# Scattering a PEER gate as two float32r parts in one product of 256 columns, with the one-hots scaled on GpSimd

## The chip, the cores and the metric

The kernel runs on one core of a Trainium2 chip. The metric is the device time of one execution in microseconds, the median of several. Engines are named as in the profile: PE is TensorE (PEld its weight loads), DVE is VectorE, ACT is ScalarE, POOL is GpSimd, and SP issues the transfers.

## What is computed

Four decoder layers work on 256 tokens of 1024 features. Each layer has an attention mixer (sliding window, dilated, latent, then sliding window again), a layer norm, a PEER channel mixer, and a second layer norm. The change touches the PEER mixer only:

```python
q = (t @ w_q).reshape(n_tok, 8, 2, 128)
sc = einsum('thpd,hpkd->thpk', q, keys)            # 128 keys per half
s_top, i_top = top_k(sc, 16)
cand = s_top[:, :, 0, :, None] + s_top[:, :, 1, None, :]
best, sel = top_k(cand, 16)                         # of 16 x 16 sums
idx = take(i_top[..., 0] * 128 + i_top[..., 1], sel)
gate = softmax(best)                                # 8 heads x 16 per token
h = gelu(einsum('cd,ced->ce', t, u[idx]))
y = einsum('ce,ced->cd', gate * h, v[idx])
```

There are 16384 experts in a 128 x 128 grid. The kernel does not gather them: it computes the hidden units of all experts for all tokens, multiplies them by a dense table of gates that is zero where an expert was not chosen, and multiplies by all of v.

## The kernel before

Matrix products that need accuracy are made of float32r parts: a weight chunk of 128 x 1024 is loaded into a raw tile (`_load`, on SP, three buffers), ACT rounds it to its high part (line 88), and DVE, or POOL for a share of the chunks (`pool_share`), subtracts to get the low part (line 94). `split_to` runs this two chunks ahead of use. A projection (`proj_t`, line 121) is then 3 x 8 matmuls of 256 columns: high by high, low by high, high by low.

One PEER layer (`peer`) has these stages, in an order that is written out by hand:

1. Scores (`peer_scores`): 16 projections of w_q chunks, products with the keys, and a copy into `sc`.
2. The hidden-unit loop, 128 iterations, one grid row of u each. Each iteration splits a chunk, projects it, and ACT applies GELU into the table G, which has the row first and the token last (G0 for rows 0 to 63, G1 for the rest).
3. The output loop, 128 iterations over v: ACT and DVE split a row of G (lines 961, 962), and PE accumulates y in four PSUM banks (lines 131 to 135).
4. The last rows with the layer norm (`sum_norm`), which adds y to x.

Beside stages 1 and 2 a generator yields small pieces of other work, and `pace` takes from it as much as a budget allows. First it is `topk_gen`: DVE finds the top 16 and the gates and writes `tab`, 128 x 3 x 256: for each of the 128 picks (partition) and each token its grid row, its grid column and its gate. `tab` is a tile of its own. When `topk_gen` ends, `weights_gen` takes its place until the end of stage 2, at `67 / (125 - j)` pieces per iteration. Of the 128 iterations of a layer, 57 come before any gate is there.

`weights_gen` turns `tab` into dense gates, four tokens (a unit) at a time, 64 units a layer. `build` makes two one-hot tiles, 128 picks by 4 tokens by 128 positions, with one compare on DVE (line 869), and multiplies the second by the gates on DVE (line 871). For each token PE multiplies the two, in plain f32 with 128 columns (line 885), which gives that token's 128 x 128 gate grid in PSUM; the trace holds two records for each such product. Units rotate through four PSUM banks. One iteration later `keep` uses the grid: rows of G that are not computed yet get the gates by a copy on ACT (line 910), and one more iteration later the rows that are computed are multiplied by them on DVE, with one input in PSUM (line 917). Where gates are there already when a row is computed, GELU goes to a temporary tile (line 941) and DVE multiplies into G afterwards (line 924, the late multiply).

SBUF is full but for little: x (128 x 2 x 1024) is held from one norm to the next though a PEER layer reads it only at its end, in the norm; its transposed parts zh and zl feed the projections.

Of the kernel before, what the change touches and what calls it, by code (L numbers as in the profile page):

```python
# [10 lines left out]
F32 = mybir.dt.float32  # L11
F32R = mybir.dt.float32r
# [3 lines left out]
AF = mybir.ActivationFunctionType  # L16
OP = mybir.AluOpType
# [4 lines left out]
T = 256  # L22
# [19 lines left out]
class Kernel:  # L42
# [674 lines left out]
            self.paced -= c  # L717
        return False

    def peer_scores(self, i):  # L720
        nc = self.nc
        keys = self.carve(16, 128)
        qT = self.ring(4, T)
        nc.sync.dma_start(keys, self.a["peer_keys"][i])

        def scores(hp2):
            p = self.small((128, 2, 2, 128))
            for q in range(2):
                hp = 2 * hp2 + q
                for t in range(2):  # L730
                    nc.tensor.matmul(p[:, t, q, :], qT[hp % 4][:, t * 128:t * 128 + 128], keys[:, hp, :],
                                     start=True, stop=True)
            nc.scalar.activation(self.sc[:, :, 2 * hp2:2 * hp2 + 2, :], p, AF.Copy)

        for hp in range(16):
            self.xproj(qT[hp % 4])
            if hp % 2 == 0 and hp:
                scores(hp // 2 - 1)
                self.sc_ready = hp - 2
            self.pace(1.3)  # L740
        scores(7)
        self.sc_ready = 16

    def topk_gen(self, tab):

        nc = self.nc
        V = nc.vector
# [28 lines left out]
        for t in range(2):  # L776
# [3 lines left out]
            f = sif.rearrange("p (h q) k -> p h q k", q=2)  # L780
# [68 lines left out]
            yield 0.2  # L849
        yield 0  # L850
        yield 0
        for t in range(2):
            p = self.small((128, 4, 128))
            for q in range(3):
                nc.tensor.transpose(p[:, q, :], stk[:, t, q, :], self.ident)
            V.tensor_copy(tab[:, 0:3, t * 128:t * 128 + 128], p[:, 0:3, :])
            yield 0.2

    def weights_gen(self, tab, keep):

        nc = self.nc
        V = nc.vector
        shape = [128, 2, 4, 128]
        units = {}

        def build(u):
            ts = slice(4 * u, 4 * u + 4)
            ab = self.misc.tile(shape, F32, name="wk", bufs=2)
            V.tensor_tensor(ab, self.iota[:, None, None, :].to_broadcast(shape),  # L869
                            tab[:, 0:2, ts][:, :, :, None].to_broadcast(shape), op=OP.is_equal)  # L870
            V.tensor_mul(ab[:, 1], ab[:, 1], tab[:, 2, ts][:, :, None].to_broadcast([128, 4, 128]))  # L871
            units[u] = ab

        build(0)
        yield 1
        kept, due = None, None
        for u in range(66):
            if u + 1 < 64:
                build(u + 1)
            p = None  # L880
            if u < 64:
                p = self.ps.tile([128, 4, 128], F32, name=f"y{u % 4}", bufs=1)
                ab = units.pop(u)
                for k in range(4):
                    nc.tensor.matmul(p[:, k, :], ab[:, 0, k, :], ab[:, 1, k, :], start=True, stop=True)  # L885
            if due is not None:
                due()
            due = keep(4 * u - 4, kept.rearrange("p t j -> p j t")) if kept is not None else None
            kept = p
            yield 1  # L890

    def peer(self, i, turn):
        nc = self.nc
        self.new_work()
        tab = self.misc.tile([128, 3, T], F32, name="tab", bufs=1)
        self.sc = self.carve(2, 16, 128)
        self.sc_ready, self.paced = 0, 0.0
        self.side = self.topk_gen(tab)
        self.pool_share = 0.2
        self.peer_scores(i)  # L900
        G = [self.big.tile([128, 64, T], F32, name="G0", bufs=1), None]
        done = [0, 0]

        def keep(t0, p):

            ts = slice(t0, t0 + 4)
            n = [min(max(done[0] - 64 * f, 0), 64) for f in range(2)]
            for f in range(2):
                if n[f] < 64:
                    nc.scalar.activation(G[f][:, n[f]:64, ts], p[:, 64 * f + n[f]:64 * f + 64, :], AF.Copy)  # L910
            done[1] = t0 + 4

            def due():
                for f in range(2):
                    if n[f]:
                        g = G[f][:, 0:n[f], ts]
                        nc.vector.tensor_mul(g, g, p[:, 64 * f:64 * f + n[f], :])
            return due

        started = False  # L920
        late = iter(())

        def times(g, tmp, td):
            nc.vector.tensor_mul(g[:, 0:td], g[:, 0:td], tmp[:, 0:td])
            yield 1

        rate = 1.3
        for j in range(128):
            hi, lo = self.r8(self.nxt())
            ps = self.hps()  # L930
            self.proj_t(ps, hi, lo, self.zh, self.zl, 8)
            if j == 64 and not started:
                self.pace(9999)
                G[1] = self.big.tile([128, 64, T], F32, name="G1", bufs=1)
            next(late, 0)
            late = iter(())
            g = G[j // 64][:, j % 64, :]
            td = done[1]
            if td:
                tmp = self.misc.tile([128, T], F32, name="gtmp", bufs=2)  # L940
                nc.scalar.activation(tmp[:, 0:td], ps[:, 0:td], AF.Gelu)  # L941
                if td < T:
                    nc.scalar.activation(g[:, td:T], ps[:, td:T], AF.Gelu)
                late = times(g, tmp, td)
            else:
                nc.scalar.activation(g, ps, AF.Gelu)  # L946
            done[0] = j + 1
            if self.pace(rate) and not started:
                started = True
                self.pool_share = 0.2  # L950
                if G[1] is None:
                    G[1] = self.big.tile([128, 64, T], F32, name="G1", bufs=1)
                self.side, self.paced = self.weights_gen(tab, keep), 0.0
                rate = 67.0 / (125 - j)
        next(late, 0)
        self.pace(9999)

        def split_g(j):
            gz = self.misc.tile([128, 4, T], F32R, name="wk", bufs=2)
            g = G[j // 64][:, j % 64, :]  # L960
            nc.scalar.activation(gz[:, 0, :], g, AF.Copy)  # L961
            nc.vector.tensor_sub(gz[:, 1, :], g, gz.bitcast(F32)[:, 0, :])  # L962
            return gz[:, 0, :], gz[:, 1, :]

        self.pool_share = 0.0
        self.y = self.psy()
        n = 128 - YTAIL
        z = split_g(0)
        for j in range(n):
            hi, lo = self.nxt(min(SPLITAHEAD, n - 1 - j))  # L970
            if j == n - 1:
                self.new_z()
                for k in range(YTAIL - 3):
                    self.split_to(self.n_use + k, [q[:, 4 * k:4 * k + 4].rearrange("p a b -> p (a b)")
                                                   for q in (self.zh, self.zl)])
            zn = split_g(j + 1) if j < n - 1 else None
            self.proj_n(self.y, hi, lo, z[0], z[1], j == 0, False)
            z = zn
            if j == 67:
                self.new_aux()  # L980
            if j in (68, 71, 74, 77):
                k = (j - 68) // 3
                self.load_norms(i, nc.sync, slice(k, k + 1))
            if j in (80, 83, 86, 89):
                k = (j - 80) // 3
                self.load_biases(i + 1, nc.sync, slice(k, k + 1))
            if j >= 100:
                self.mask_biases(1)
        w = []
        for k in range(0, YTAIL, 2):  # L990
            m = min(2, YTAIL - k)
            if m == 2:
                gz = self.misc.tile([128, 2, 2, T], F32R, name="wk", bufs=2)
                gh, gl = gz[:, 0], gz[:, 1]
            else:
                gh, gl = [self.misc.tile([128, 1, T], F32R, name="gtmp", bufs=2) for _ in range(2)]
            g = G[1][:, 64 - YTAIL + k:64 - YTAIL + k + m, :]
            nc.scalar.activation(gh, g, AF.Copy)
            nc.vector.tensor_sub(gl, g, gh.bitcast(F32))  # L999
            for q in range(m):  # L1000
                w.append(self.nxt(min(SPLITAHEAD, YTAIL - 1 - k - q)) + (gh[:, q], gl[:, q]))
        self.sum_norm(w, False, True, self.ln_slice(0), turn)
# [209 lines left out]
```

## Time and profile before

| | us |
|---|---|
| median of 3 executions | 3997.79 |
| lowest to highest | 3996.78 to 3998.18 |
| the profiled execution | 4000.66 |
| its span | 3998.8 |
| PE busy | 3934.8 |
| DVE busy | 3017.9 |
| ACT busy | 1894.6 |
| POOL busy | 336.1 |

The profile is one execution. A busy engine runs an instruction of the kernel; its durations overlap within PE, so that the spacing of starts tells more about PE than the length of one matmul. DVE instructions overlap a little too: the next starts when the one before is nearly over. An instruction that is held by something other than a semaphore shows it as a longer duration. Stretches are counted from the span's start; the granted clock of 1.00 is TensorE at 2.4 GHz. Below, a line of order of time is the start, the length and the instruction, several alike merged with their count.

### The profile page before, as it was taken

How to read it: one execution, taken by the hardware profiler on the slowest of the kernel's cores; microseconds unless marked ns; L12 is line 12 of the kernel's file. 1: busy time of each engine (PE TensorE's matmuls, PEld its weight loads, DVE VectorE, ACT ScalarE, POOL GpSimd, SP SyncE). 2: the span in 40 equal slices, each digit the busy share in tenths (PEclk: the TensorE clock that was granted, in tenths of full speed). 3: DMA queues.
4: the chain of work that ended last, by engine and by line, in shares of the span. 5: the costliest groups of instructions: out<-in, count | busy, mean ns of one | idle time of the engine just before them, and what ended most of it. 6: DMA issues, size and time to landing. Idle time of an engine off the chain costs nothing. (4 is left out here: it accounts for less than half of the span.)

```text
span 3998.8 us, 68740 instructions
## 1 busy us (share of the span) xinstructions
PE 3934.8 (98%) x26592; PEld 3579.7 (90%) x26592; DVE 3017.9 (75%) x5798; ACT 1894.6 (47%) x3568; POOL 336.1 (8%) x135
## 2 busy tenths in 40 slices
PE   8999999999999999999999999999999999999999
PEld 6999998888998999988887999998888899998887
DVE  7888985566667989965557888985566788996555
ACT  5444444445554444444445444434445444444444
POOL 0111110000001111100000111110000111110000
PEclk9999999999999999999999999999999999999999
DMA  5454445564444554455653554445564455445554
GB/s 182 161 185 151 143 148 187 203 215 156 140 143 143 175 174 143 138 169 189 215 182 105 169 183 152 143 142 187 197 221 148 143 181 168 143 138 175 189 199 159
DMA packets 188007, 668.00 MB, mean 167 GB/s; under 512 B 20688, under 2 KB 27408, under 8 KB 187168
## 3 DMA queue, kind: packets, MB, share of 16 engines
q1 hardware_dynamic: 187424, 663.46, 49.8%
q8 instruction: 209, 3.42, 0.3%
q14 instruction: 118, 0.97, 0.1%
q0 software_dynamic: 64, 0.08, 0.0%
q10 hardware_dynamic: 192, 0.07, 0.0%
HBM read 662.46 MB, written 1.07 MB: 166 GB/s over the span
## 5 line engine op out<-in xcount | busy, mean ns | idle before, releaser
L94 DVE TENSOR_TENSOR lo<-raw,hi 128x1024 fp32r<-128x1024 f32 x1083 | 1324.3, 1223 | 825.4 <-ACT hi L88 821.7
L88 ACT ACTIVATE hi<-raw 128x1024 fp32r<-128x1024 f32 x1212 | 1281.3, 1058 | 724.6 <-PE y L135 696.3
L121 PE MATMUL hp<-zh,hi 128*128 128x256 f32 x5360 | 784.5, 289 | 2.5 <-ACT zh L222 1.7
L121 PE MATMUL hp<-zh,lo 128*128 128x256 f32 x5360 | 752.6, 283 | 0.0
L121 PE MATMUL hp<-zl,hi 128*128 128x256 f32 x5360 | 751.3, 283 | 0.0
L121 PEld LDWEIGHTS hp<-zh,hi 128*128 128x128 f32 x5360 | 689.4, 192 | 9.6 <-issue 4.5
L121 PEld LDWEIGHTS hp<-zh,lo 128*128 128x128 f32 x5360 | 691.7, 192 | 0.0
L121 PEld LDWEIGHTS hp<-zl,hi 128*128 128x128 f32 x5360 | 691.4, 192 | 0.0
L133 PE MATMUL y<-lo,wk 128*128 128x512 f32 x2004 | 632.5, 396 | 0.0
L131 PE MATMUL y<-hi,wk 128*128 128x512 f32 x2004 | 629.0, 394 | 3.5 <-ACT wk L961 3.3
L135 PE MATMUL y<-hi,wk 128*128 128x512 f32 x2004 | 631.8, 396 | 0.2 <-DVE wk L999 0.2
L94 POOL TENSOR_TENSOR lo<-raw,hi 128x1024 fp32r<-128x1024 f32 (+1 forms) x129 | 334.7, 2596 | 3293.6 <-ACT hi L88 3090.5
L131 PEld LDWEIGHTS y<-hi,wk 128*128 128x128 f32 x2004 | 375.7, 188 | 96.6 <-ACT wk L961 4.1
L135 PEld LDWEIGHTS y<-hi,wk 128*128 128x128 f32 x2004 | 376.0, 188 | 93.3 <-DVE wk L999 0.6
L133 PEld LDWEIGHTS y<-lo,wk 128*128 128x128 f32 x2004 | 376.2, 188 | 89.2
L941 ACT ACTIVATE gtmp<-hp 128x256 f32<-128x256 f32 (+52 forms) x284 | 80.6, 284 | 615.3 <-PE hp L121 313.6
L869 DVE TENSOR_TENSOR wk<-iota,tab 128x1024 f32<-128x1024 f32 x256 | 314.1, 1227 | 0.1
L885 PE MATMUL y<-wk 128*128 128x128 f32 x2048 | 271.1, 275 | 13.5 <-DVE wk L871 13.5
L885 PEld LDWEIGHTS y<-wk 128*128 128x128 f32 x2048 | 250.2, 192 | 15.7 <-DVE wk L871 15.7
L871 DVE TENSOR_TENSOR wk<-wk,tab 128x512 f32<-128x512 f32 x256 | 245.7, 960 | 8.8
L946 ACT ACTIVATE G<-hp 128x256 f32<-128x256 f32 x228 | 87.6, 384 | 340.9 <-PE hp L121 340.6
L962 DVE TENSOR_TENSOR wk<-G,wk 128x256 fp32r<-128x256 f32 x492 | 206.0, 419 | 2.4 <-ACT wk L961 2.4
(190 smaller groups left out, 2686.0 us busy)
## 6 DMA issues: line engine op xcount, KB each, us to landing
raw<-in_peer_u SPq DMA_DIRECT2D x512, 512.0 KB, 3.3
raw<-in_peer_v SPq DMA_DIRECT2D x512, 512.0 KB, 3.3
raw<-in_dil_w SPq DMA_DIRECT2D x72, 512.0 KB, 3.6
raw<-in_peer_wq SPq DMA_DIRECT2D x64, 512.0 KB, 3.6
raw<-in_swa_w SPq DMA_DIRECT2D x20, 512.0 KB, 4.0
G<-in_lnp SPq DMA_DIRECT2D x16, 512.0 KB, 4.6
raw<-in_swa_wo SPq DMA_DIRECT2D x16, 512.0 KB, 3.5
G<-relb SPq DMA_DIRECT2D x12, 512.0 KB, 4.7
```

The lines of the kernel that those rows point to most:

```text
L88: nc.scalar.activation(h[:, :w], r[:, :w], AF.Copy)
L94: eng.tensor_sub(lo[:, :w], r[:, :w], h.bitcast(F32)[:, :w])
L121: mm(ps, w[:, k, :], z[:, k0 + k, :], start=(p == 0 and k == 0), stop=(p == 2 and k == nk - 1))
L131: mm(ps[t][b][:, :s.stop - s.start], zh[:, ts], hi[:, s], start=first, stop=False)
L133: mm(ps[t][b][:, :s.stop - s.start], zh[:, ts], lo[:, s], start=False, stop=False)
L135: mm(ps[t][b][:, :s.stop - s.start], zl[:, ts], hi[:, s], start=False, stop=last)
L869: V.tensor_tensor(ab, self.iota[:, None, None, :].to_broadcast(shape), tab[:, 0:2, ts][:, :, :, None].to_broadcast(shape), op=OP.is_equal)
L871: V.tensor_mul(ab[:, 1], ab[:, 1], tab[:, 2, ts][:, :, None].to_broadcast([128, 4, 128]))
L885: nc.tensor.matmul(p[:, k, :], ab[:, 0, k, :], ab[:, 1, k, :], start=True, stop=True)
L941: nc.scalar.activation(tmp[:, 0:td], ps[:, 0:td], AF.Gelu)
L946: nc.scalar.activation(g, ps, AF.Gelu)
L962: nc.vector.tensor_sub(gz[:, 1, :], g, gz.bitcast(F32)[:, 0, :])
```

## The change

- `build` compares into a float32r tile of three parts: the row one-hot in part 0 and the column one-hot in part 2. POOL then scales the column one-hot, token by token and part by part, with eight `tensor_scalar` instructions of 128 elements: part 1 gets it times the gate's high part, part 2 in place times the low part. DVE's multiply of line 871 is gone.
- PE makes for each token one float32r product of 256 columns: row one-hot by the two scaled ones side by side. A unit takes two PSUM banks, so that two units fit in four banks.
- A new step `add` comes one iteration later: ACT copies the low halves from PSUM to an SBUF tile (two instructions of 256 elements), and DVE adds the high halves from PSUM (two instructions). `keep` comes one iteration later still and reads SBUF where it read PSUM. The generator has 68 pieces.
- `topk_gen` rounds the gate to its high part and subtracts to get the low part (two more steps per token half), so the table has four rows per token.
- The table (4 x 256) and the two SBUF sums (512 each) take exactly x's place: at the sixth of the 16 score projections SP sends x to a DRAM tile, the table is laid in the same tile name, and at iteration 92 of the output loop SP brings x back.

```diff
         for hp in range(16):
...
+            if hp == 5:
+                lend()
...
-            V.tensor_copy(tab[:, 0:3, t * 128:t * 128 + 128], p[:, 0:3, :])
-            yield 0.2
-
-    def weights_gen(self, tab, keep):
+            ts = slice(t * 128, t * 128 + 128)
+            V.tensor_copy(tab[:, 0:2, ts], p[:, 0:2, :])
+            yield 0.2
+            V.tensor_copy(tab.bitcast(F32R)[:, 2, ts], p[:, 2, :])
+            yield 0.2
+            V.tensor_sub(tab[:, 3, ts], p[:, 2, :], tab[:, 2, ts])
+            yield 0.2
+
+    def weights_gen(self, tab, sums, keep):
...
         def build(u):
-            ts = slice(4 * u, 4 * u + 4)
-            ab = self.misc.tile(shape, F32, name="wk", bufs=2)
-            V.tensor_tensor(ab, self.iota[:, None, None, :].to_broadcast(shape),
-                            tab[:, 0:2, ts][:, :, :, None].to_broadcast(shape), op=OP.is_equal)
-            V.tensor_mul(ab[:, 1], ab[:, 1], tab[:, 2, ts][:, :, None].to_broadcast([128, 4, 128]))
+            ab = self.misc.tile([128, 3, 4, 128], F32R, name="wk", bufs=2)
+            V.tensor_tensor(ab[:, 0:3:2], self.iota[:, None, None, :].to_broadcast(shape),
+                            tab[:, 0:2, 4 * u:4 * u + 4][:, :, :, None].to_broadcast(shape), op=OP.is_equal)
+            one = ab.bitcast(F32)[:, 2]
+            for k in range(4):
+                for q in range(2):
+                    nc.gpsimd.tensor_scalar(ab[:, 1 + q, k, :], one[:, k, :], tab[:, 2 + q, 4 * u + k:4 * u + k + 1], 1.0,
+                                            op0=OP.mult, op1=OP.mult)
             units[u] = ab
+
+        def products(u):
+            ab = units.pop(u)
+            ps = [self.ps.tile([128, 2, 2, 128], F32, name=f"y{2 * (u % 2) + e}", bufs=1) for e in range(2)]
+            for k in range(4):
+                nc.tensor.matmul(ps[k // 2][:, k % 2], ab[:, 0, k, :], ab[:, 1:3, k, :], start=True, stop=True)
+            return ps
+
+        def add(u, ps):
+            p = sums[u % 2]
+            for e in range(2):
+                nc.scalar.activation(p[:, 2 * e:2 * e + 2], ps[e][:, :, 1, :], AF.Copy)
+            for e in range(2):
+                s = p[:, 2 * e:2 * e + 2]
+                V.tensor_add(s, s, ps[e][:, :, 0, :])
+            return p
...
-        for u in range(66):
+        for u in range(67):
             if u + 1 < 64:
                 build(u + 1)
-            p = None
-            if u < 64:
-                p = self.ps.tile([128, 4, 128], F32, name=f"y{u % 4}", bufs=1)
-                ab = units.pop(u)
-                for k in range(4):
-                    nc.tensor.matmul(p[:, k, :], ab[:, 0, k, :], ab[:, 1, k, :], start=True, stop=True)
+            ps = products(u) if u < 64 else None
             if due is not None:
                 due()
-            due = keep(4 * u - 4, kept.rearrange("p t j -> p j t")) if kept is not None else None
-            kept = p
+            due = keep(4 * u - 8, summed.rearrange("p t j -> p j t")) if summed is not None else None
+            summed = add(u, fresh) if fresh is not None else None
+            fresh = ps
             yield 1
...
+        def lend():
+            nc.sync.dma_start(xs, self.x)
+            z = self.misc.tile([128, 2048], F32, name="x", bufs=1)
+            lent.append(z[:, 0:1024].rearrange("p (q t) -> p q t", q=4))
+            lent.append([z[:, 1024 + 512 * e:1536 + 512 * e].rearrange("p (t j) -> p t j", t=4) for e in range(2)])
...
-                rate = 67.0 / (125 - j)
+                rate = 68.0 / (125 - j)
...
+            if j == 92:
+                self.x = self.misc.tile([128, 2, 1024], F32, name="x", bufs=1)
+                nc.sync.dma_start(self.x, xs)
```

## Rows read from the trace of the kernel before

**Rows 1.** The page's first part: busy time, share, instructions of each engine.
```profile
PE 3934.8 (98%) x26592; PEld 3579.7 (90%) x26592; DVE 3017.9 (75%) x5798; ACT 1894.6 (47%) x3568; POOL 336.1 (8%) x135
```

**Rows 2.** Stretches: start:end, length, busy PE, PEld, DVE, ACT, POOL (instructions), clock, DMA.
```profile
200.00:300.00 100.00, 100.00 (x835) 100.00 (x835) 83.87 (x202) 45.91 (x69) 18.30 (x7) 1.00 0.56 185
400.00:500.00 100.00, 100.00 (x851) 100.00 (x850) 98.30 (x148) 42.12 (x106) 14.41 (x6) 1.00 0.43 143
500.00:560.00 60.00, 57.51 (x486) 57.10 (x485) 58.79 (x86) 22.93 (x63) 7.92 (x3) 1.00 0.41 133
```

**Rows 3.** The stretch 400 to 500 again, line 121 alone, then line 885 alone.
```profile
400.00:500.00 100.00, 83.83 (x651) 79.42 (x650) 1.00 0.43 143
400.00:500.00 100.00, 26.29 (x200) 24.38 (x200) 1.00 0.43 143
```

**Rows 4.** PE in order of time, gate group to gate group: start, length.
```profile
404.46 1.05 PE L885 MATMUL y<-wk 128*128 128x128 f32 x8
405.26 1.20 PE L121 MATMUL hp<-zh,hi 128*128 128x256 f32 x8
...
408.22 1.05 PE L885 MATMUL y<-wk 128*128 128x128 f32 x8
```

**Rows 5.** DVE in order of time, from one compare to the next.
```profile
457.00 1.21 DVE L869 TENSOR_TENSOR wk<-iota,tab 128x1024 f32<-128x1024 f32 x1
458.24 0.69 DVE L871 TENSOR_TENSOR wk<-wk,tab 128x512 f32<-128x512 f32 x1
458.85 0.60 DVE L917 TENSOR_TENSOR G<-G,y 128x256 f32<-128x256 f32 x2
459.37 1.22 DVE L94 TENSOR_TENSOR lo<-raw,hi 128x1024 fp32r<-128x1024 f32 x1
460.50 0.30 DVE L924 TENSOR_TENSOR G<-G,gtmp 128x140 f32<-128x140 f32 x1
460.72 1.22 DVE L869 TENSOR_TENSOR wk<-iota,tab 128x1024 f32<-128x1024 f32 x1
```

**Rows 6.** DVE in order of time late in the stage, two compares.
```profile
535.84 1.22 DVE L869 TENSOR_TENSOR wk<-iota,tab 128x1024 f32<-128x1024 f32 x1
...
539.74 1.22 DVE L869 TENSOR_TENSOR wk<-iota,tab 128x1024 f32<-128x1024 f32 x1
```

**Rows 7.** DVE and ACT forms of 256 columns: busy us, mean ns, idle.
```profile
L917 DVE TENSOR_TENSOR G<-G,y 128x256 f32<-128x256 f32 x228 | 94.5, 414 | 0.0
L946 ACT ACTIVATE G<-hp 128x256 f32<-128x256 f32 x228 | 87.6, 384 | 340.9 <-PE hp L121 340.6
```

**Rows 8.** DVE and POOL in order of time, around 399 and around 455 us.
```profile
398.81 1.22 DVE L869 TENSOR_TENSOR wk<-iota,tab 128x1024 f32<-128x1024 f32 x1
400.06 2.76 DVE L871 TENSOR_TENSOR wk<-wk,tab 128x512 f32<-128x512 f32 x1
398.92 3.36 POOL L94 TENSOR_TENSOR lo<-raw,hi 128x1024 fp32r<-128x1024 f32 x1 [15.53 <-DVE G L924]
...
454.49 2.43 POOL L94 TENSOR_TENSOR lo<-raw,hi 128x1024 fp32r<-128x1024 f32 x1 [16.43 <-ACT hi L88]
455.09 1.98 DVE L924 TENSOR_TENSOR G<-G,gtmp 128x136 f32<-128x136 f32 x1
```

**Rows 9.** Single lines: duration in ns, least/median/most, first and last start, forms.
```profile
L871 DVE TENSOR_TENSOR wk<-wk,tab x256: 691/692/2942, 312.5 to 3611.3; 128x512 f32<-128x512 f32 x128
L917 DVE TENSOR_TENSOR G<-G,y x480: 146/400/419, 323.6 to 3621.5; 128x256 f32<-128x256 f32 x72, 128x228 f32<-128x228 f32 x4, 128x240 f32<-128x240 f32 x4, 128x252 f32<-128x252 f32 x4
L94 POOL TENSOR_TENSOR lo<-raw,hi x129: 1807/2410/3402, 90.1 to 3628.3; 128x1024 fp32r<-128x1024 f32 x127, 128x768 fp32r<-128x768 f32 x2
```

**Rows 10.** POOL's other forms: busy, mean ns, idle before.
```profile
L94 POOL TENSOR_TENSOR lo<-raw,hi 128x768 fp32r<-128x768 f32 x2 | 3.6, 1824 | 366.6 <-ACT hi L88 366.6
L1205 POOL MEMSET const-float32-0.0<- 128x1 f32 x1 | 0.1, 98 | 0.2 <-issue 0.2
```

**Rows 11.** DMA issues of the page or its view: count, KB, us to landing.
```profile
G<-in_peer_keys SPq DMA_DIRECT2D x4, 1024.0 KB, 5.7
```

More of the change, by code (lines that the diff above doesn't have):

```diff
@@ L718, in pace, with peer_scores @@
         return False
-    def peer_scores(self, i):
+    def peer_scores(self, i, lend):
         nc = self.nc
@@ L851, in topk_gen @@
         yield 0
+        tab = tab()
         for t in range(2):
@@ L874, in weights_gen @@
         build(0)
         yield 1
-        kept, due = None, None
-        for u in range(66):
+        fresh, summed, due = None, None, None
+        for u in range(67):
             if u + 1 < 64:
                 build(u + 1)
-            p = None
-            if u < 64:
-                p = self.ps.tile([128, 4, 128], F32, name=f"y{u % 4}", bufs=1)
-                ab = units.pop(u)
-                for k in range(4):
-                    nc.tensor.matmul(p[:, k, :], ab[:, 0, k, :], ab[:, 1, k, :], start=True, stop=True)
+            ps = products(u) if u < 64 else None
@@ L894, in peer @@
         self.new_work()
-        tab = self.misc.tile([128, 3, T], F32, name="tab", bufs=1)
+        xs = self.dram.tile([128, 2, 1024], F32, name="xs")
+        lent = []
+        def lend():
[3 more added lines that the diff above has]
+            lent.append([z[:, 1024 + 512 * e:1536 + 512 * e].rearrange("p (t j) -> p t j", t=4) for e in range(2)])
         self.sc = self.carve(2, 16, 128)
         self.sc_ready, self.paced = 0, 0.0
-        self.side = self.topk_gen(tab)
+        self.side = self.topk_gen(lambda: lent[0])
         self.pool_share = 0.2
-        self.peer_scores(i)
+        self.peer_scores(i, lend)
         G = [self.big.tile([128, 64, T], F32, name="G0", bufs=1), None]
@@ L952, in peer @@
                     G[1] = self.big.tile([128, 64, T], F32, name="G1", bufs=1)
-                self.side, self.paced = self.weights_gen(tab, keep), 0.0
-                rate = 67.0 / (125 - j)
+                self.side, self.paced = self.weights_gen(lent[0], lent[1], keep), 0.0
+                rate = 68.0 / (125 - j)
         next(late, 0)
```

## The prediction

> **What bounds the kernel now.** I read the share of each engine first: PE is busy for 98% of the span, so time can come back only where PE's own work shrinks, and can be lost wherever something makes PE wait [rows 1]. The next view is the table of stretches, since the change touches one stage of each layer, the hidden-unit loop while gates are scattered. The reader is to see there that PE is the bound before this stage (DVE at 84% from 200 to 300) and that inside it PE and DVE run level: DVE is busy for 98.3 of the 100 us from 400 to 500, and from 500 to 560 it is even fuller (58.79 of 60) than PE (57.51) [rows 2]. ACT has more than half of its time free, POOL 85%.
>
> From 400 to 500 PE did 651 matmuls of line 121, 24 to an iteration, so 27.1 iterations, and 200 records of line 885, eight to a unit of four tokens, so 25 units [rows 3]. An iteration takes 100 / 27.1 = 3.69 us and holds 0.92 units. Without units it takes 24 x 100 / 835 = 2.87 us [rows 2], so a unit costs PE (100 - 27.1 x 2.87) / 25 = 0.89 us. The order of time agrees: from the gate group at 404.46 to the next is 3.76, of which the group holds 0.80 before the next projection starts [rows 4].
>
> DVE's own order of time is the more important view. One iteration with a unit runs without a gap: compare 1.24, gate multiply 0.61, two keep multiplies 0.52, a low-part subtraction 1.13, the late multiply 0.22, together 3.72 [rows 5]. Later, when the multiplies cover more columns, the same round takes 3.90 [rows 6], more than PE's 3.76. Per iteration DVE is busy 98.30 / 27.1 = 3.63 of 3.69 us.
>
> **The change part by part.** *PE.* Four products of 128 columns in f32 become four of 256 columns in float32r, the very form of line 121, which costs 2.87 / 24 = 0.12 each. A unit should take 0.48, with the switch between kinds about 0.50, so PE alone would need 2.87 + 0.92 x 0.50 = 3.33 per iteration. That is 0.39 less for each of 256 units, 100 us, if PE stayed the bound.
>
> *DVE.* The compare keeps its 1024 elements. The gate multiply goes: 0.92 x 0.61 = 0.56 less. Two additions of 256 elements with one PSUM input come: between 0.30 each (the gap between 1024 and 512 elements in rows 5, 0.63, is 1.23 ns an element) and 0.41 each (the same form in rows 7); I take 0.33, so 0.92 x 0.66 = 0.61 more (0.55 to 0.76). DVE stands at 3.63 - 0.56 + 0.61 = 3.68 (3.62 to 3.83). So DVE alone holds the iteration where it is, and PE's 0.36 buys next to nothing. This is the first step of my forecast.
>
> *POOL.* Eight scalings of 128 elements per unit, 7.4 per iteration, join the 0.2 subtractions. No row shows such an operation. The floor is a memset's 0.10; the ceiling is an eighth of the 1024-element subtraction, 0.30, plus 0.10 [rows 9, 10]. I take 0.25, nearer to neither; then POOL is busy 7.4 x 0.25 + 0.2 x 2.41 = 2.3 of 3.7 us (1.2 to 3.4), which fits if nothing holds it up.
>
> But something does. At 398.92 POOL's subtraction starts while DVE's compare runs (398.81 to 400.03) and takes 3.36 us in place of 2.41; DVE's gate multiply starts at 400.06 and ends only at 402.82, 0.54 after POOL: 2.76 us for 0.69 of work. At 455.09 a late multiply takes 1.98 in the same way [rows 8]. The keep multiply, whose one input lies in PSUM, never takes more than 0.42 in 480 times, while the gate multiply with two SBUF inputs goes up to 2.94 [rows 9]. So a POOL operation and a DVE operation with two SBUF inputs exclude each other. The Trainium skill says so as a rule (SBUF — State Buffer, "Who interferes with whom"): whichever starts first keeps the shared port for the whole instruction, and a VectorE instruction with two SBUF inputs contends with any GpSimd instruction that reads SBUF. The trace agrees with it for POOL's subtraction (2.76 against 0.69); that a scaling with one tensor input counts too stands only in the rule.
>
> If scalings do exclude, DVE has 4.6 such operations an iteration (0.92 compares, 1.84 keep multiplies, which lose their PSUM input by this change, 0.8 subtractions, one late multiply) and they would alternate with POOL's. By rows 8 a POOL operation that already waits hides 2.41 - 2.25 = 0.16 of itself, and the DVE operation behind it hides 0.18 (it ended 2.79 after the compare, 2.25 of it POOL's, against 0.72 when nothing is in its way). At 0.25 a scaling then costs DVE nothing, at 0.40 0.07: 0 to 0.32 an iteration, and I take 0.12, since tidy turns will not always come. The other price is turns: POOL gets about 4.6, and 0.61 / 0.25 = 2.4 more beside the additions, 7.0 of its 7.4, with the 2.41 us subtraction in the same queue. I take 0.15 for what DVE must stand idle (0 to 0.50, the latter with 0.40 a scaling).
>
> *Waits.* Behind the product that waits for POOL stand the 24 matmuls of the next projection, and so GELU on ACT and the late multiply on DVE. A unit is built one iteration ahead, 3.7 us of cover for 8 x 0.25 = 2.0 of scaling plus turns; gone, each late us is PE's. PSUM holds two units instead of four, so a product also waits for the additions of two units before, an iteration's slack. ACT gets two copies of 0.38 [rows 7], 0.71 an iteration on an engine at 42%: nothing.
>
> *x.* Four times 1 MB goes out during the scores and comes back in the output loop, all on SP's queue before weight loads. A 1 MB load lands in 5.7 us [rows 11]; exposed in full, eight would cost 46 us. I take nothing: three raw buffers and splits two chunks ahead stand between a late load and PE. The four extra table steps per layer are below 1 us of DVE while DVE has 16% free.
>
> **The sum.** 3.68 + 0.12 + 0.15 = 3.95 against 3.69, 0.26 more. A layer has 64 / 0.92 = 69.5 such iterations, four layers 278: 72 us. The profiled span of 3998.8 becomes 4071; that execution took 4000.66, 2.9 above the median of 3997.79, so the median becomes 4070. The upper ends, 3.83 + 0.32 + 0.50 = 4.65, give 267 more, 4265; the lower end of the DVE term, 3.62, with nothing excluded gives 19 less, 3979.
>
> **The rivals.** *POOL becomes the bound (slower still).* If a scaling takes 0.40 or turns go badly, the iteration is 4.4 to 4.8 and the time 4195 to 4305. For it: POOL's ordinary rate of 2.4 ns an element. Against: it has one input, not two. *Scalings don't exclude, and DVE has air (faster).* The decisive point is whether DVE gets below 3.6. With keep multiplies shorter from SBUF and additions at 0.30, DVE may run at 3.4 to 3.6: 25 to 80 us less, 3918 to 3973. Against it stands the 3.90 of rows 6. *PE's gain is real but DVE keeps the pace (no change).* Iteration 3.66 to 3.72: 3990 to 4006. *The change doesn't do what it says*: the products do not run like line 121 but like the old ones. With DVE the bound this alters little and sits inside the cases.
>
> **How the numbers follow.** Slower as summed, 4006 to 4190: 0.52. POOL as bound: 0.18. Faster: 0.21. No change: 0.09. The range leaves out the top of the POOL case and the far end of the faster one: 3955 to 4270. The measurement of this kernel can tell about 0.2% (8 us) from no change, so faster 0.21, same 0.09, slower 0.70.
>
> **What would show it.** Right: the gate group on PE at about 0.5; DVE at or near 100% of the stage; compares and subtractions stretched by parts of a us, keep multiplies too, additions not; idle PE before the gate product that ends on POOL or DVE; POOL at 60% or more there. Wrong: scalings that run beside two-input DVE work unhurt, DVE below 95%, or an iteration at 3.4. A granted clock below 1.00 in the stage would mean that PE's waits had grown far beyond these sums.

## The result and the profile after

The changed kernel takes 4567.64 us against 3997.95 for the one before: a ratio of 1.1421, with a 95% interval of 1.1399 to 1.1444. One of its four executions took 6083.84 us at a mean granted clock of 0.588, and the ratio leaves it out. The direction was forecast, the size was not: 570 us slower, where 72 were expected and 272 was the end of the range. The profiled execution of after took 4567.46, its span 4565.7.

The page of after, against [rows 1]: PE's busy time, then the busy tenths of POOL and the granted TensorE clock in 40 slices of the span.

```profile
PE 4129.0 (90%) x25568; PEld 3684.0 (81%) x25568; DVE 3092.8 (68%) x6070; ACT 2090.1 (46%) x4072; POOL 1598.5 (35%) x2183
...
POOL 0138881000001178950000138881000117896000
PEclk9998889999999988889999998889999998888999
```

POOL went from 336 to 1598 us. Its four busy stretches are the four gate stages, and in the same slices the clock falls to eight tenths. PE is busy for longer in all (4129 against 3935), though it has less to do, since it runs slower there.

Two stretches of the first gate stage, with the columns of [rows 2]:

```profile
400.00:500.00 100.00, 77.46 (x485) 72.16 (x485) 66.84 (x113) 40.66 (x100) 87.49 (x138) 0.84 0.28 91
500.00:600.00 100.00, 76.91 (x488) 71.69 (x486) 70.58 (x113) 38.98 (x102) 91.38 (x131) 0.85 0.26 87
```

Before, PE and DVE ran level at 98 to 100%. Now both have room (PE 77%, DVE 67 to 71%) and POOL is at 87 to 91%. The bound has moved to POOL.

The first and last gate product of the first layer, before:

```profile
L885 PEld LDWEIGHTS y<-wk x512: 186/192/192, 314.8 to 567.5; 128*128 128x128 f32 x171
```

and after:

```profile
L890 PEld LDWEIGHTS y<-wk x256: 186/188/330, 316.7 to 704.4; 128*128 128x128 f32 x128
```

The stage was 252.7 us long and is 387.7. Summed over the four layers, from first to last product, it went from 1016 to 1564 us, 547 of the 567 us between the two spans. The other 20 us lie outside these bounds and were not traced further. From 400 to 600 the trace has 840 projection matmuls in 200 us, 35 iterations of 5.71 us where 3.69 stood.

POOL's scaling and who waited for it (least/median/most ns; us and times):

```profile
L882 POOL TENSOR_SCALAR wk<-wk,x x2048: 362/372/2462, 313.8 to 4178.7; 128x128 fp32r<-128x128 f32 x187
...
  PEld y L890: 472.6, 415
  PE y L890: 381.0, 372
```

and by form (busy us, mean ns, idle before) the scaling, the compare (now, and before the change) and the keep multiply of 256 columns, with the addition of 256 columns (least/median/most ns):

```profile
L882 POOL TENSOR_SCALAR wk<-wk,x 128x128 fp32r<-128x128 f32 x2048 | 1282.7, 637 | 188.0 <-DVE wk L877 92.5
...
L877 DVE TENSOR_TENSOR wk<-iota,x 128x1024 fp32r<-128x1024 f32 x256 | 327.6, 1280 | 35.2 <-PE y L890 35.0
...
L869 DVE TENSOR_TENSOR wk<-iota,tab 128x1024 f32<-128x1024 f32 x256 | 314.1, 1227 | 0.1
...
L949 DVE TENSOR_TENSOR G<-G,x 128x256 f32<-128x256 f32 x232 | 142.0, 612 | 0.0
...
L899 DVE TENSOR_TENSOR x<-x,y x512: 411/419/427, 325.6 to 4184.7; 128x256 f32<-128x256 f32 x171
```

A scaling takes 0.372 us when nothing holds it, but 0.637 on average: 0.265 x 2048 = 543 us of POOL's 1283 is holding. The compare is hardly hurt: 1.280 on average, 1.227 before. In the trace 574 of the 2048 scalings take over 0.4 us, and each of these runs beside a DVE operation with two operands in SBUF (compare, subtraction, keep or late multiply). The 569 that run beside nothing but an addition, whose second operand lies in PSUM, take 0.379 at most, and no addition takes more than 0.427. PE's sequence at one unit that waits and, ahead of it, at one that does not, in order of time (start, length, idle and releaser):

```profile
348.07 0.63 PE L890 MATMUL y<-wk 128*128 128x256 f32 x4
348.54 1.12 PE L121 MATMUL hp<-zh,hi 128*128 128x256 f32 x8
...
455.83 0.38 PE L890 MATMUL y<-wk 128*128 128x256 f32 x1 [0.43 <-POOL wk L882]
...
457.57 0.58 PE L890 MATMUL y<-wk 128*128 128x256 f32 x1 [1.36 <-POOL wk L882]
...
457.95 1.91 PE L121 MATMUL hp<-zh,hi 128*128 128x256 f32 x8
...
459.66 1.91 PE L121 MATMUL hp<-zh,lo 128*128 128x256 f32 x8
...
463.68 1.12 PE L121 MATMUL hp<-zh,hi 128*128 128x256 f32 x8
...
464.64 1.12 PE L121 MATMUL hp<-zh,lo 128*128 128x256 f32 x8
```

At the later unit PE stands and waits for POOL at each product; then the projection runs at the lower of the clock's two levels (eight matmuls in 1.71 us from 457.95 to 459.66, granted clock 0.50, 1.2 GHz), and after a stretch without waits at the higher one again (0.96 from 463.68 to 464.64, granted clock 1.00, 2.4 GHz). The four products themselves take 0.47 when nothing makes them wait (348.07 to 348.54, granted clock 1.00).

### The profile page after: what moved, and what is told of

Same layout as the page of the kernel before. It is cut to its first block, busy times and chain, and to the rows that moved or that the text cites. A ratio compares the mean times of both kernels' runs of the same rounds, so it can differ in the third digit from the quotient of the medians.

```text
span 4565.7 us, 69785 instructions
## 1 busy us (share of the span) xinstructions
PE 4129.0 (90%) x25568; PEld 3684.0 (81%) x25568; DVE 3092.8 (68%) x6070; ACT 2090.1 (46%) x4072; POOL 1598.5 (35%) x2183
## 5 line engine op out<-in xcount | busy, mean ns | idle before, releaser
L94 DVE TENSOR_TENSOR lo<-raw,hi 128x1024 fp32r<-128x1024 f32 x1083 | 1354.2, 1251 | 916.7 <-ACT hi L88 913.9
L88 ACT ACTIVATE hi<-raw 128x1024 fp32r<-128x1024 f32 x1212 | 1281.1, 1058 | 730.6 <-PE y L135 696.6
L882 POOL TENSOR_SCALAR wk<-wk,x 128x128 fp32r<-128x128 f32 x2048 | 1282.7, 637 | 188.0 <-DVE wk L877 92.5
L94 POOL TENSOR_TENSOR lo<-raw,hi 128x1024 fp32r<-128x1024 f32 (+1 forms) x129 | 317.4, 2463 | 2410.2 <-ACT hi L88 2396.7
L121 PE MATMUL hp<-zh,lo 128*128 128x256 f32 x5360 | 820.7, 300 | 0.0
L121 PEld LDWEIGHTS hp<-zh,hi 128*128 128x128 f32 x5360 | 755.2, 208 | 9.6 <-issue 4.5
L121 PEld LDWEIGHTS hp<-zh,lo 128*128 128x128 f32 x5360 | 762.1, 210 | 0.0
L890 PE MATMUL y<-wk 128*128 128x256 f32 x1024 | 298.1, 355 | 383.5 <-POOL wk L882 381.0
L890 PEld LDWEIGHTS y<-wk 128*128 128x128 f32 x1024 | 183.9, 207 | 474.6 <-POOL wk L882 472.6
L899 DVE TENSOR_TENSOR x<-x,y 128x256 f32<-128x256 f32 x512 | 192.5, 417 | 378.5 <-ACT x L896 378.5
L973 ACT ACTIVATE gtmp<-hp 128x4 f32<-128x4 f32 (+13 forms) x280 | 79.3, 283 | 714.6 <-PE hp L121 698.0
L877 DVE TENSOR_TENSOR wk<-iota,x 128x1024 fp32r<-128x1024 f32 x256 | 327.6, 1280 | 35.2 <-PE y L890 35.0
L896 ACT ACTIVATE x<-y 128x256 f32<-128x256 f32 x512 | 168.9, 385 | 240.5 <-DVE G L949 240.5
```

The lines of the kernel that those rows point to most:

```text
L88: nc.scalar.activation(h[:, :w], r[:, :w], AF.Copy)
L94: eng.tensor_sub(lo[:, :w], r[:, :w], h.bitcast(F32)[:, :w])
L121: mm(ps, w[:, k, :], z[:, k0 + k, :], start=(p == 0 and k == 0), stop=(p == 2 and k == nk - 1))
L877: V.tensor_tensor(ab[:, 0:3:2], self.iota[:, None, None, :].to_broadcast(shape), tab[:, 0:2, 4 * u:4 * u + 4][:, :, :, None].to_broadcast( ...
L882: nc.gpsimd.tensor_scalar(ab[:, 1 + q, k, :], one[:, k, :], tab[:, 2 + q, 4 * u + k:4 * u + k + 1], 1.0, op0=OP.mult, op1=OP.mult)
L890: nc.tensor.matmul(ps[k // 2][:, k % 2], ab[:, 0, k, :], ab[:, 1:3, k, :], start=True, stop=True)
```

## The experiments

Two theories stood against each other first: A, POOL's scalings are the bound; B, the longer chain behind the product (copies, additions, two units in PSUM) is. C asked for the clock's part.

**Without scalings.** The product reads the unscaled one-hot twice.

```diff
-            for k in range(4):
-                for q in range(2):
-                    nc.gpsimd.tensor_scalar(ab[:, 1 + q, k, :], ...)
...
-                nc.tensor.matmul(..., ab[:, 1:3, k, :], start=True, stop=True)
+                nc.tensor.matmul(..., ab[:, 2, k, :][:, None, :].to_broadcast([128, 2, 128]), start=True, stop=True)
```

> The changed kernel without the eight scalings on GpSimd: the product reads the unscaled column one-hot twice, so the gates are left out of the result. All else of the change stays (float32r product of 256 columns, copies on ACT, additions on DVE, two units in PSUM, x in DRAM). Theory A (GpSimd's scalings, 5.0 us busy a unit, are the bound): the stage falls back to what DVE needs, 3.6 to 3.8 us an iteration, 3975 to 4040 us in all, with the clock back at 1.00. Theory B (the longer chain of copies, additions and PSUM tiles is what stretches it): above 4300 us.

Measured: 4297.14, ratio 1.0745 (1.0713 to 1.0776). Neither theory fits: the time is 257 us above what A allowed and 3 below what B did. 270 us go with the scalings, but 299 remain. The stretch from 400 to 500 shows PE at 78%, DVE at 83%, POOL at 12%, so that no engine is full:

```profile
400.00:500.00 100.00, 78.28 (x573) 74.81 (x572) 83.31 (x135) 45.94 (x117) 12.00 (x4) 0.95 0.33 108
```

and one round in order of time shows why:

```profile
453.24 1.06 ACT L88 ACTIVATE hi<-raw 128x1024 fp32r<-128x1024 f32 x1
...
454.33 1.23 DVE L94 TENSOR_TENSOR lo<-raw,hi 128x1024 fp32r<-128x1024 f32 x1 [0.47 <-ACT hi L88]
...
455.48 0.26 DVE L952 TENSOR_TENSOR G<-G,gtmp 128x104 f32<-128x104 f32 x1
455.65 1.22 DVE L877 TENSOR_TENSOR wk<-iota,x 128x1024 fp32r<-128x1024 f32 x1
...
456.79 0.83 DVE L945 TENSOR_TENSOR G<-G,x 128x256 f32<-128x256 f32 x2
457.71 0.66 ACT L892 ACTIVATE x<-y 128x256 f32<-128x256 f32 x2 [2.67 <-DVE G L945]
...
458.25 1.06 ACT L88 ACTIVATE hi<-raw 128x1024 fp32r<-128x1024 f32 x1
```

Each line begins where the one before ends, across engines: ACT rounds a chunk (L88), DVE subtracts it (L94), does the late multiply (L952), the compare (L877) and the keep multiplies (L945), then ACT may copy (L892), because it writes into the sum tile that those multiplies read, and only after that it rounds the next chunk. From 453.24 to 458.25 is 5.01 us, a closed ring between two engines. I call it theory D; it is a chain of the kind that B named.

**The order of scalings.** High parts first, then low parts.

```diff
-            for k in range(4):
-                for q in range(2):
+            for q in range(2):
+                for k in range(4):
```

> The changed kernel with the two loops of the scalings exchanged: first the four high parts, then the four low parts in place. In the trace every second scaling waits for the one before it, because it overwrites what that one reads: starts are 0.346 us apart without this wait and 0.465 with it. Theory A (GpSimd is the bound and works through its queue without a pause): 4 x 0.12 = 0.48 us less for each of 256 units, 120 us, so 4420 to 4480 us. Theory B (chain of copies and additions): 4540 to 4570 us, no change.

Measured: 4476.74, ratio 1.1194 (1.1161 to 1.1226), 91 us less. In the trace the starts of scalings that nothing else holds now lie 0.35 apart throughout.

```profile
L882 POOL TENSOR_SCALAR wk<-wk,x 128x128 fp32r<-128x128 f32 x2048 | 1285.6, 646 | 89.2 <-DVE wk L877 89.2
```

POOL's idle time before its scalings was 188.0 us in the changed kernel, 92.5 of it for the compare. The other 95.5, its waits for itself, are gone here. About three quarters of the 120 us arrive, since no more than these 95.5 were there to be saved; POOL's busy time is nearly the same (1285.6 against 1282.7). POOL's time is the kernel's time, as A says.

**Fillers on PE.**

```diff
+            f = self.small()[:, :T]
+            for k in range(16):
+                nc.tensor.matmul(f, self.zh[:, k % 8, 0:128], self.zh[:, k % 8, :], start=(k == 0), stop=(k == 15))
```

> The changed kernel with 16 more float32r matmuls of 256 columns (0.12 us each at 2.4 GHz, 1.9 us a unit) into a scratch PSUM tile ahead of each unit's products, where PE otherwise waits for GpSimd; nobody reads them. It asks what the lower clock of the stage (granted 0.80 to 0.89) costs. Theory A with the clock as a mere companion: PE's waits swallow them, 4540 to 4600 us. Theory C (the half clock, at which eight matmuls of a projection take 1.70 us instead of 0.96, is a large part of the loss): granted clock back near 1.00 and 4350 to 4480 us. If PE has no real slack: up to 490 us more.

Measured: 4581.56, ratio 1.1456 (1.1423 to 1.1489), 14 us more than the changed kernel. The stretch from 500 to 600:

```profile
500.00:600.00 100.00, 95.03 (x753) 93.28 (x752) 70.28 (x115) 40.98 (x105) 92.59 (x133) 0.97 0.27 88
```

The clock is back at 0.97 (0.85 before the fillers), and the time is not. PE is 95% busy with the fillers, but it still waits for POOL before the products, 107 us in all (381 without fillers), and POOL is about as busy as without them (93% against 91). So the lower clock is a companion of PE's waiting and not what sets the time. C falls.

**One size.** Two scalings of 512 in place of eight of 128.

```diff
-            for k in range(4):
-                for q in range(2):
-                    nc.gpsimd.tensor_scalar(ab[:, 1 + q, k, :], one[:, k, :], tab[:, 2 + q, 4 * u + k:4 * u + k + 1], 1.0,
-                                            op0=OP.mult, op1=OP.mult)
+            for q in range(2):
+                nc.gpsimd.tensor_scalar(ab[:, 1 + q], one, tab[:, 2 + q, 4 * u:4 * u + 1], 1.0,
+                                        op0=OP.mult, op1=OP.mult)
```

> The changed kernel with two scalings of 512 elements a unit in place of eight of 128; all four tokens get the gate of the first, so the result is not the reference's. One size is changed: it tells the fixed part of a scaling from its part per element. If the 0.372 us of a scaling is nearly all fixed, 512 elements take 0.4 to 0.7 us; if it is 0.1 fixed and 2.1 ns an element, 1.2 us. Theory A: GpSimd's own work a unit falls from 3.24 us to 0.8 to 2.4 us, and it queues behind DVE two times instead of eight; 4050 to 4350 us. Theory B: above 4500 us.

Measured: 4310.77, ratio 1.0779 (1.0747 to 1.0810). The scaling of 512:

```profile
L881 POOL TENSOR_SCALAR wk<-wk,x x512: 687/701/2754, 313.4 to 3923.4; 128x512 fp32r<-128x512 f32 x171
```

384 elements more cost 0.701 - 0.372 = 0.329 us, so, if the time grows evenly with the elements, 0.86 ns an element on 0.26 fixed. Seven tenths of a small scaling is fixed cost. POOL is no longer the bound here (1.4 us a unit before holding), and the time stops 14 us above the run without scalings: at the ring.

**A third sum tile, without scalings.** The one-hot tile is smaller here, which makes the place.

```diff
-            ab = self.misc.tile([128, 3, 4, 128], F32R, name="wk", bufs=2)
+            ab = self.misc.tile([128, 2, 4, 128], F32R, name="wk", bufs=2)
...
-            lent.append([z[:, 1024 + 512 * e:1536 + 512 * e].rearrange("p (t j) -> p t j", t=4) for e in range(2)])
+            lent.append([z[:, 1024 + 512 * e:1536 + 512 * e].rearrange("p (t j) -> p t j", t=4) for e in range(2)]
+                        + [self.misc.tile([128, 4, 128], F32, name="s3", bufs=1)])
...
-            p = sums[u % 2]
+            p = sums[u % 3]
```

> As the run without scalings (gates left out of the result), with a third sum tile, so that ACT's copy into a sum tile no longer waits for DVE's keep multiplies of the same iteration. Theory D: in the run without scalings the time is set by a ring: ACT copies low halves, then rounds the next chunk (1.06), DVE subtracts it (1.2), does the late multiply (0.2), the compare (1.24), the two keep multiplies (0.83), and these let ACT copy again (0.54): 5.0 us, with neither engine full. Without that wait DVE's own work is left, about 4.1 us an iteration (keep multiplies are longer from SBUF): 4080 to 4160 us. Rival: the two PSUM units or the additions set it: 4270 to 4300, unchanged.

Measured: 4022.20, ratio 1.0062 (1.0041 to 1.0082), 275 us less than with two tiles. The ring is shown, and what lies under it is the next bound:

```profile
400.00:500.00 100.00, 92.70 (x717) 88.11 (x717) 100.00 (x167) 59.73 (x151) 18.33 (x6) 1.00 0.42 133
```

DVE has no free moment left, PE is at 93%. An iteration (619 projection matmuls, 25.8 in 100 us) takes 3.88.

**The keep multiplies first, full kernel.**

```diff
+            if due is not None:
+                due()
             if u + 1 < 64:
                 build(u + 1)
             ps = products(u) if u < 64 else None
-            if due is not None:
-                due()
```

> The changed kernel, whole, with one exchange: the keep multiplies of a unit are issued ahead of the next compare instead of behind it. This takes the compare (1.24 us) out of the ring of theory D (5.0 to about 3.8 us), and leaves GpSimd's scalings as they are. If GpSimd alone sets the changed kernel (theory A): 4530 to 4570. If the ring and GpSimd add up: 4250 to 4400.

Measured: 4610.33, ratio 1.1533 (1.1510 to 1.1556).

**The third sum tile, full kernel.** It takes the place of the masks, which come again by a load in the output loop.

```diff
-            lent.append([z[:, 1024 + 512 * e:1536 + 512 * e]... for e in range(2)])
+            m = self.misc.tile([128, 1024], F32, name="masks", bufs=1)
+            lent.append([s.rearrange(...) for s in (z[:, 1024:1536], z[:, 1536:2048], m[:, 0:512])])
...
-            p = sums[u % 2]
+            p = sums[u % 3]
```

> The changed kernel, whole, with the third sum tile (in the place of the masks, which are loaded again in the output loop), so that ACT's copies no longer wait for the keep multiplies: the ring is cut, GpSimd's scalings stay as they are. If GpSimd alone sets the changed kernel: 4520 to 4570, at most 50 less. If the ring's 275 us lie on top of GpSimd's part: 4280 to 4320.

Measured: 4597.69, ratio 1.1498 (1.1479 to 1.1517). This run cuts the ring and the one before shortens it, and neither gains: in the changed kernel the ring lies inside the time that POOL needs. Theory A holds for the whole. But both are slower than the changed kernel, by 30 us here and 43 with the keep multiplies first, and so outside what was expected. The third-tile run's compare, what it waited for, and who waited for it (us, times), and the scalings of this run and of the one with the keep multiplies first:

```profile
  PE y L890: 123.5, 87
...
  POOL wk L882: 143.2, 48
...
L882 POOL TENSOR_SCALAR wk<-wk,x 128x128 fp32r<-128x128 f32 x2048 | 1260.6, 626 | 238.7 <-DVE wk L877 143.2
...
L882 POOL TENSOR_SCALAR wk<-wk,x 128x128 fp32r<-128x128 f32 x2048 | 1226.3, 609 | 284.0 <-DVE wk L877 188.5
```

In the changed kernel the two waits were 35.0 and 92.5. DVE comes to its compare before PE has released the one-hot tile, and POOL waits for the compare: 51 us more here, 96 more with the keep multiplies first. Some of it comes back, since the scalings are held less. POOL's busy and idle time together rises from 1470.7 to 1499.3 and to 1510.3, by 29 and 40 us, which is nearly the loss of 30 and 43. No run takes this wait away alone, so its cause stays read, not shown.

**Two large products on POOL.** With the keep multiplies first.

```diff
-            for k in range(4):
-                for q in range(2):
-                    nc.gpsimd.tensor_scalar(...)
+            for q in range(2):
+                nc.gpsimd.tensor_tensor(ab[:, 1 + q], one, tab[:, 2 + q, 4 * u:4 * u + 4][:, :, None].to_broadcast([128, 4, 128]), op=OP.mult)
```

> As the run with the keep multiplies first, with the scalings as two GpSimd products of 512 elements a unit, two SBUF inputs each (the gates read with a step of zero), about 1.2 us each by half of the 1024-element subtraction. The result is whole. GpSimd's own work falls from 3.24 to 2.4 us a unit. If its time and the time of DVE's two-input work simply add up at the shared SBUF port (2.6 us DVE and 0.92 x 2.4 + 0.5 GpSimd an iteration): about 5.3 us an iteration, 4380 to 4480. If DVE's work runs beside it: near 4120 to 4200.

Measured: 4373.47, ratio 1.0940 (1.0918 to 1.0962), 7 us under the expected stretch and 237 under the run with the keep multiplies first, from which it differs in the scalings alone. From 500 to 600:

```profile
500.00:600.00 100.00, 74.72 (x528) 71.22 (x527) 99.99 (x124) 43.67 (x113) 60.67 (x40) 0.91 0.31 100
```

Here both engines are held: DVE shows 100% busy, with its compare at 1.479 on average, and POOL, at 61%, takes 1.413 on average for a product that takes 1.04 when nothing holds it. An iteration takes 5.22 us (919 projection matmuls from 400 to 600). POOL alone needs 0.94 x 2 x 1.04 + 0.2 x 2.41 = 2.4 an iteration; with 3.1 for DVE's work on two SBUF operands (reckoned below) the sum is 5.5. The two come near to adding up. Why DVE is held so much more here than in the changed kernel was not tested; POOL's operations are longer (1.04 against 0.372).

**Memsets for scalings.** POOL writes the same 128 elements and reads nothing.

```diff
-                    nc.gpsimd.tensor_scalar(ab[:, 1 + q, k, :], ...)
+                    nc.gpsimd.memset(one[:, 1 + q, k, :], 1.0)
```

> The changed kernel with each of the eight scalings replaced by a GpSimd memset of the same 128 elements of the same tile, with the same waits on the compare; the gates are left out of the result. A memset writes SBUF and reads nothing. In the changed kernel 30% of the scalings take over 0.4 us, up to 2.4, where 0.37 is the ordinary length. If they are held because they read SBUF while a DVE operation with two SBUF inputs runs (shared port), memsets are never held: all of one length of 0.1 to 0.3 us, and the ring alone is left, 4285 to 4320 us as without scalings. If any GpSimd operation is held by DVE: long ones remain and the time stays above 4400.

Measured: 4298.26, ratio 1.0752 (1.0730 to 1.0773), the ring's time. All 2048 of them:

```profile
L882 POOL MEMSET wk<- x2048: 194/204/223, 309.5 to 3904.8; 128x128 f32 x187
```

None is held: 0.194 to 0.223, where scalings at the same place, with the same wait for the compare, went from 0.36 to 2.46. A memset differs from a scaling in that it reads nothing, so what holds POOL is its reading of SBUF, and by the counts above it is held while DVE reads two operands there.

**x alone**, in the kernel before.

```diff
+            if hp == 5:
+                nc.sync.dma_start(xs, self.x)
...
+            if j == 92:
+                self.x = self.misc.tile([128, 2, 1024], F32, name="x", bufs=1)
+                nc.sync.dma_start(self.x, xs)
```

> The kernel before with one part of the change alone: x is written to DRAM at the sixth score projection and read back at iteration 92 of the output loop, four times 1 MB each way; table and gates as before. Prediction's step: hidden, 3990 to 4006. Exposed in full by the 5.7 us of a 1 MB load: up to 4044.

Measured: 3998.40, ratio 1.0003 (0.9993 to 1.0012). Hidden, as predicted.

**A version without POOL.**

```diff
+            V.tensor_tensor(ab[:, 0], iota..., tab[:, 0, ...]..., op=OP.is_equal)
+            for k in range(4):
+                for q in range(2):
+                    V.tensor_scalar(ab[:, 1 + q, k, :], self.iota, tab[:, 1, c], tab[:, 2 + q, c], op0=OP.is_equal, op1=OP.mult)
...
-                self.pool_share = 0.2
+                self.pool_share = 0.0
...
-            p = sums[u % 2]
+            p = sums[u % 3]
...
-            due = keep(4 * u - 8, summed.rearrange("p t j -> p j t")) if summed is not None else None
+            due = keep(4 * u - 8, summed) if summed is not None else None
```

> A version that takes the experiments' lessons: the float32r product of 256 columns stays; GpSimd does nothing in the gate stage (no scalings, no subtractions); DVE makes the row one-hot by a compare of 512 elements (0.61) and each scaled column one-hot by one operation with two per-token scalars (equal to the column, times the gate part; 8 of 128 elements a unit); three sum tiles (the third in the place of the masks, which are loaded again in the output loop), with the token innermost, so that keep multiplies read runs of four. The price of the fused operation is in no row: at 0.15 us an iteration needs 3.3 to 3.5 us of DVE and 3.35 of PE: 3920 to 3960. At 0.27 us: 4.3 us, 4150 to 4190.

Measured: 4300.00, ratio 1.0757 (1.0739 to 1.0775), above both prices. DVE's order of time, and behind it a pair of keep multiplies of the run with the third sum tile and no scalings:

```profile
449.06 0.42 DVE L956 TENSOR_TENSOR G<-G,gtmp 128x96 f32<-128x96 f32 x1
449.23 0.86 DVE L877 TENSOR_TENSOR wk<-iota,x 128x512 fp32r<-128x512 f32 x1
449.83 2.31 DVE L882 TENSOR_SCALAR wk<-iota,x 128x128 fp32r<-128x128 f32 x8
451.88 0.74 DVE L949 TENSOR_TENSOR G<-G,x 128x256 f32<-128x256 f32 x2
452.36 0.92 DVE L898 TENSOR_TENSOR x<-x,y 128x256 f32<-128x256 f32 x2
453.02 1.40 DVE L94 TENSOR_TENSOR lo<-raw,hi 128x1024 fp32r<-128x1024 f32 x1
...
450.82 0.88 DVE L946 TENSOR_TENSOR G<-G,s 128x256 f32<-128x256 f32 x2
451.62 0.73 DVE L895 TENSOR_TENSOR x<-x,y 128x256 f32<-128x256 f32 x2
```

Eight fused operations take 2.05 us (449.83 to 451.88), 0.26 each, behind a compare of 0.60; before the change compare and gate multiply took 1.85 in all [rows 5], and the additions come on top. DVE is busy for all of the 100 us from 400 to 500, and an iteration takes 4.97 (966 projection matmuls from 400 to 600), where 4.3 was reckoned for about this price. The other new layout helped: the pair of keep multiplies takes 0.48 from its start to the additions for 332 columns (451.88 to 452.36), where it took 0.80 for 364 (450.82 to 451.62). The pair of additions takes 0.66 (452.36 to 453.02).

**POOL's old share, in the kernel before.**

```diff
-                self.pool_share = 0.2
+                self.pool_share = 0.0
```

> The kernel before with GpSimd's share of the subtractions at zero in the gate stage in place of 0.2. It prices the exclusion where it was already: an iteration wins 0.38 us of DVE being held and pays 0.2 x 1.13 more subtraction. DVE falls from 3.63 to about 3.5 us an iteration, below PE's 3.69; only the late part, where DVE was the bound, gets shorter: 3980 to 3996.

Measured: 3981.47, ratio 0.9960 (0.9946 to 0.9974): 16 us faster than the kernel before, and the best of all.

```profile
400.00:500.00 100.00, 100.00 (x851) 100.00 (x851) 94.49 (x155) 42.16 (x106) 0.00 (x0) 1.00 0.44 143
500.00:560.00 60.00, 60.00 (x512) 60.00 (x511) 58.71 (x92) 23.94 (x63) 0.00 (x0) 1.00 0.44 141
...
L871 DVE TENSOR_TENSOR wk<-wk,tab x256: 691/692/696, 312.5 to 3593.8; 128x512 f32<-128x512 f32 x128
```

Against [rows 2] DVE's busy time fell from 98.30 to 94.49 of 100 though it does a quarter more subtractions, and PE has no idle time left from 500 to 560 (57.51 before). The gate multiply, which took up to 2.942 [rows 9], never takes more than 0.696. The same exclusion that sinks the change was already costing something.

## Why the prediction was right and wrong

*PE and DVE run level, so PE's gain buys nothing: right.* Without scalings and without the ring the kernel is at 4022, with DVE full. The DVE term was a little small: 3.88 us an iteration measured, 3.68 (3.62 to 3.83) forecast. The additions fit (0.66 a pair in the version without POOL). What was missing is that the keep multiply does not only lose its freedom from POOL when it moves to SBUF, but reads there with a step of 512 bytes: 0.612 us on average for 256 columns against the 0.414 of [rows 7], which has the same step in PSUM.

*The gate group at 0.50: right, where nothing makes it wait.* It is 0.47 from the first product to the projection (348.07 to 348.54), 0.80 before by the same measure [rows 4].

*The price of a scaling: taken too low.* 0.25 was taken between 0.10 and 0.40; it is 0.372, and every second one waits 0.12 for the one before it, whose input it overwrites. A pair spans 0.81, so a unit is 3.24 us of POOL without any holding, not 2.0.

*Exclusion: the kind was right, the sum was the step that failed.* The prediction read from [rows 8] that a waiting operation hides 0.16 to 0.18 of itself, concluded that a held operation costs 0 to 0.07, and counted turns. It reckoned what a scaling costs DVE, and gave POOL's turns a number but no length: a scaling that arrives behind a compare or a subtraction waits for as much of 1.2 us as is left. POOL paid 0.265 a scaling, DVE nearly nothing. The two terms, 0.12 for the exclusion and 0.15 for the turns, stood for 0.27 us an iteration. The runs put 1.83 in their place: 5.71 in the changed kernel less the 3.88 that is left without scalings and without the ring. Adding the users of the port would have come much closer: per iteration 7.5 x 0.372 + 0.2 x 2.41 = 3.3 of POOL's, and 0.94 x (1.22 + 0.8) + 0.8 x 1.22 + 0.25 = 3.1 of DVE's compares, keep multiplies, subtractions and late multiplies, are 6.4, against 5.71 measured and 3.95 forecast. The Trainium skill's rule (SBUF — State Buffer, "Who interferes with whom") was the right guide for this: the run with memsets confirms the part that the trace before could not show, that a POOL operation which only writes is not held (0.223 at most), and the scalings that one with a single tensor input is.

*The rival "POOL becomes the bound": the right mechanism, at 4195 to 4305 mis-sized.* It let an iteration grow to 4.8 at most, because it took the ceiling of a scaling as its price and left the holding where the main sum had it. The iteration is 5.71.

*ACT's copies for nothing: wrong, but not what set the result.* The look at ACT's load (42%) missed that a copy into one of only two sum tiles has to wait for DVE, and that ACT's next rounding stands behind it. Alone this ring costs 275 us (4297 to 4022). In the changed kernel POOL covers it, as the runs that cut it show.

*The clock.* A clock below 1.00 was named as the sign of waits far beyond the sums; it came, and the fillers show that giving it back gains nothing here. Of the other signs, PE's waits for POOL, unstretched additions and POOL above 60% came too. DVE at or near 100% did not: at 67 to 71% it is below the 95% that was named as a sign of being wrong. *x* was hidden, as forecast.

So the 570 us divide, by differences of runs, into 24 for DVE as the bound, 275 more for the ring, 270 more for POOL's scalings. They do not add as separate costs: each bound lies over the one below, and POOL's alone would give the whole.

## What to carry to other kernels

Before work is handed to GpSimd, add its SBUF-reading time to VectorE's two-input time of the same stretch: where the sum exceeded the period here, the period became 0.89 and 0.95 of that sum (5.71 of 6.4, 5.22 of 5.5), and in the changed kernel the engine with the many short operations paid. Follow each new tile's write-after-read through the order of both engines' queues, because a ring of waits can set the time where no engine is full (DVE 83%, PE 78%). A product that got cheaper on TensorE was worth nothing here while VectorE ran level with it.

## What the runs showed of the hardware

GpSimd's `tensor_scalar` of 128 columns takes 0.372 us, of 512 columns 0.701, a memset of 128 columns 0.204. A wait for GpSimd's own previous operation spreads two starts from 0.346 to 0.465 us. VectorE's operation with two per-token scalars takes 0.26 us from start to start for 128 columns: eight of them took 2.05, while one broadcast compare of 512 columns took 0.60. A VectorE multiply that reads one operand in SBUF with a step of 512 bytes took 0.61 us on average for 256 columns (0.58 at least), and with the same step in PSUM 0.41. Four float32r products of 256 columns with one-hot weights took 0.47 us at a granted clock of 1.00, 0.12 each as in the projections, where the four plain f32 products of 128 columns took 0.80.
